# Output-gate projections of a gated recurrence as seven-product blocks of head pairs

## The chip, the cores and the metric

One of a Trainium2 chip's cores runs the kernel. TensorE (PE) multiplies, VectorE (DVE), ScalarE (ACT) and GpSimd (POOL) work on elements, SyncE (SP) and others issue the DMA transfers; each engine runs its own queue in order, and the engines wait for each other by semaphores. The metric is the device time of one execution in microseconds (us).

## The reference, cut to what matters

A residual block for 1024 tokens and 1024 channels: attention over 8 heads of 64 and a gated recurrence over 4 heads of 128 run side by side on the same normalised input, are merged by sigmoid gates, and an MLP follows.

```python
xn = rmsnorm(x, norm1_g)
q_sb, k_sb, v_sb, f_raw, i_hg, q_hg, g_hg, gate_sb, gate_hg = split(xn @ w_in)
o_sb = stick_breaking_attention(q_sb, k_sb, v_sb)
f = lb + (1 - lb) * sigmoid(f_raw)
k_hg = (1 - lb) * sigmoid(-f_raw)
o_hg = hgrn2_chunkwise(silu(q_hg), k_hg, i_hg, log(f))     # 4 heads of 128
o_hg = rmsnorm(o_hg, hg_norm_g)                            # per head
o_hg = merge_heads(o_hg) * silu(g_hg)                      # the output gate
g_a = sigmoid(gate_sb + b_a); g_b = sigmoid(gate_hg + b_b)
merged = g_a * (o_sb @ w_o_sb) + g_b * (o_hg @ w_o_hg)
h = x + merged @ w_out
h = h + square(relu(rmsnorm(h) @ w_ff1)) @ w_ff2
out = rmsnorm(h, final_g)
```

The change concerns `g_hg`, the last 512 of the recurrence's columns of `w_in`, and where its product with the head outputs is made.

## The kernel before, in words

**Numbers.** Every float32 operand of a product is split in two, a high part (a rounding copy on ScalarE, L148) and the rest (a subtraction on VectorE, L153). A product is three matmuls: high by high, high by low, low by high (`three`, L121). A matmul here has 128 rows of weights, 128 columns and 512 tokens. In names an `h` at the end is the high, an `l` the low part, `r` the raw weights as loaded. L161 is a multiplication on VectorE (`mul`), L1087 an addition, L1090 a subtraction, L124 a transpose on PE.

**Stages.** Normalisation and first projections (to about 60 us), attention (to 318), the recurrence (to 592), the rest of `o_sb @ w_o_sb` (to 615), the gates stage with `o_hg @ w_o_hg` (to 745), `w_out`, then the MLP.

**Two lanes on PE.** What depends on other engines (attention's scores and values, the recurrence's levels) is written by hand in order and goes to the lane "main". Projections that only need the normalised input are jobs of a stream `st` and go to the lane "fill": `st.advance(n, upto)` emits n steps of six matmuls each between pieces of the main lane, up to job number `upto`. Within a lane the order is that of the code, and a fill step is held behind the main block of `AHEAD = 2` blocks before, so that it runs where the main lane would leave PE idle. When a job starts, `prefetch` splits the next job's weights and loads those of the job after it.

**The recurrence.** Head h has eight levels (`hg_levels(h)`): `sd`, the diagonal, then levels 0 to 6 with doubling blocks, scores `sl` on PE and scalings of `k`, `q` and the decay `pp` on VectorE. Its tail (`hg_tail(h)`) has six parts: transposes `pk`, chunk states `pkv`, two halves of the output `pho` with their norm (`hon`, through GpSimd's `hn_y`), and two transposes back, `pot`. Levels of head h and the tail of head h-1 take turns. After every one of these parts fill steps are emitted, `FILL = (3.75, 3.3, 2.8, 2.6, 3)` of them by head. The gate `g` of a head is a projection of its own in the fill (`pjg`, weights `wg0` to `wg3`): per half of 512 tokens 8 blocks of 128 channels, 24 matmuls, then a sigmoid (ACT) and a product (DVE). The tail's last step multiplies the transposed output by the norm's weight and by `g`.

**Seven products for a block.** The columns of `gate_sb` and `gate_hg` were already made in pairs as two by two blocks: columns (two groups of 128) by channels (two halves of 512) by tokens (two halves of 512). Instead of eight block products there are seven. Three use the normalised input itself (`raw_job(cb)`, in the fill: banks `pga` and `pgq`, weights `wga`; the results go to DRAM in `pd` and `gd`). Four use sums of the input's blocks and of the weights' blocks and come in the gates stage, where `GatePair` loads the raw columns (`wg0r` and so on), subtracts and splits them (`whig`, `wlog`, `tgh`, `tgl`), loads the stored products (`pr`, `yr`) and does x6, y5, x7 and y3 (banks `gX`, `gY`, twelve matmuls each) and two products with `w_o_hg` (`late_half`, `early_half`: bank `pyh`, on the split head outputs `ahgh`, `ahgl`): 72 matmuls for one of the eight pairs. The input's sums (`gs`, `gsh`, `gsl`, by `sum_forms`) are made while `o_sb @ w_o_sb` runs (`sb_job`: bank `pys`, weights `wo00` to `wo03`, and `asbh`, `asbl` the split attention outputs). Head outputs are split whole, 1024 tokens at a time, by `a_hg.put`.

**Order.** The queues' order on ACT and DVE is set by a scheduler, except where `turns` is on or `after` adds an edge: there it is the code's. Loads go to SP's queue in the code's order. Raw weights have two buffers (tag `raw`), as have the high and the low parts (`whi`, `wlo`): a load waits until an older one has been read.

Of the kernel before, what the change touches and what calls it, by code (L numbers as in the profile page):

```python
# [19 lines left out]
P = 128  # L20
# [19 lines left out]
def kernel(  # L40
# [119 lines left out]
    def mul(out, a, b):  # L160
        return nc.vector.tensor_tensor(out=out, in0=a, in1=b, op=ALU.mult)  # L161
# [288 lines left out]
    class Stream:  # L450
        def __init__(self, eager=False):
            self.eager = eager
            self.jobs = []
            self.pos = 0
            self.gen = None
# [5 lines left out]
        def _start(self):  # L461
            units, body = self.jobs[self.pos]
            for u in units:
                u.split()
            if (self.pos > 0 or self.eager) and not units[-1].late:
                self.prefetch()
            self.gen = body()

# [50 lines left out]
    def proj_jobs(group, acts):  # L519


        def body():
            for half in range(2):
                for name, unit, ep in group:
# [249 lines left out]
    hg_sum, hg_level = [None], [None]  # L774
# [46 lines left out]
    def hg_jobs(h):  # L821
        for key, c0, ep in (
            ("f", C_F, f_epilogue(h)),
            ("q", C_QH, silu_epilogue(h, "q")),
            ("g", C_GH, silu_epilogue(h, "g")),
        ):
            if key == "g" and h % 2 == 0:
                i_job(h)
            u = cols_unit(f"w{key}{h}", [(W_IN, c0 + h * P, P)])
            j_hg[h] = proj_jobs([(f"pj{key}{h}", u, ep)], xn)  # L830

# [40 lines left out]

    def hg_levels(h):
# [17 lines left out]
        def pairs_of(name, n, *products):  # L891
# [4 lines left out]
            hi_lo(h_, l_, t)  # L896
# [28 lines left out]
        yield  # L925
        for l in range(7):
# [54 lines left out]
            yield  # L981

    def hg_tail(h):
        dec, k, q, g, v, sc = (hg.pop((h, n)) for n in ("pp", "k", "q", "g", "v", "sc"))
# [11 lines left out]
        yield  # L996
# [22 lines left out]
        yield  # L1019
        ons = []  # L1020
        for half in range(2):
# [14 lines left out]
            mul(chunks(on), chunks(po), rstd.unsqueeze(2).to_broadcast([P, 4, P]))  # L1036
            ons.append(on)
            yield
        for half, cs in halves():
            open_block("main")  # L1040
            pot = bank(f"pot{h}_{half}")
            for j in range(4):
                js = slice(j * P, (j + 1) * P)
                transpose(pot[:, js], ons[half][:, js])
            nc.vector.scalar_tensor_tensor(
                out=g[:, cs],
                in0=pot,
                scalar=prm[:, HGN + h : HGN + h + 1],
                in1=g[:, cs],
                op0=ALU.mult,  # L1050
                op1=ALU.mult,
            )
            yield
        ohg[h] = g


    class Split:
# [28 lines left out]
    def add(out, a, b):  # L1086
        return nc.vector.tensor_tensor(out=out, in0=a, in1=b, op=ALU.add)  # L1087

    def sub(out, a, b):
        return nc.vector.tensor_tensor(out=out, in0=a, in1=b, op=ALU.subtract)  # L1090
# [6 lines left out]
    yd = [dram(f"yd{cb}", [P, 2, 512]) for cb in range(KT)]  # L1097

# [26 lines left out]
    class RawUnit(Unit):  # L1125
# [4 lines left out]
        def __init__(self, cb):  # L1130
            dmas = [
                [(0, P, W_IN[:, gate_cols(w, cb)].rearrange("(k p) c -> p k c", p=P))]
                for w in range(2)
            ]
            super().__init__(f"wga{cb}", dmas)
# [20 lines left out]
    raw_units = [RawUnit(cb) for cb in range(KT)]  # L1156

    def raw_job(cb):
        u = raw_units[cb]
# [12 lines left out]
        def body():  # L1172
            p1, p14, g1 = (half(f"{n}_{cb}") for n in ("p1", "p14", "g1"))
            ps, p4 = bank(f"pga{cb}"), bank(f"pgq{cb}")
            if cb >= 6:
                load_g1(cb - 6)
            yield from steps_of(ps, 0, 0, 0, 0, True)
            nc.scalar.copy(p1, ps)
            nc.scalar.dma_start(pd[cb][:, 0, :], p1)
            if cb == 0:  # L1180
                u.split_t()
            st.prefetch()
            yield from steps_of(p4, 1, 0, 1, 4, True)
            add(p14, p1, p4)
            if cb == 3 or cb == KT - 1:
                whole_input(1, int(cb == KT - 1))
            nc.gpsimd.dma_start(pd[cb][:, 1, :], p14)
            yield from steps_of(ps, 0, 4, 0, 4, False)
# [5 lines left out]
        return st.add([u], body)  # L1194
# [8 lines left out]
    WAIT = 5  # L1203
# [7 lines left out]
    def sum_forms():  # L1211
# [30 lines left out]
        gp[0].load()  # L1242
        gp[0].load_sums()
# [6 lines left out]
        yield from range(4)  # L1250
        gp[0].split()
# [31 lines left out]
    j_raw = []  # L1283
# [9 lines left out]
    class GatePair:  # L1293
        def __init__(self, cb):
            self.cb = cb

        def load(self):
            cb = self.cb
            self.raw = [
                wpool.tile([P, 1024], F32, tag="raw", name=f"wg{cb}r{i}") for i in range(2)  # L1300
            ]
            for i, s_, which in ((0, 0, 0), (0, 1, 1), (1, 1, 1)):
                load(
                    self.raw[i][:, s_ * 512 : (s_ + 1) * 512].rearrange("p (k c) -> p k c", k=4),
                    W_IN[i * 512 : (i + 1) * 512, gate_cols(which, cb)].rearrange(
# [3 lines left out]
            self.wo = half(f"wor{cb}")  # L1309
# [11 lines left out]
        def split(self, behind=None):  # L1321
            cb = self.cb
# [4 lines left out]
            h, l = (  # L1327
                wpool.tile([P, 1024], F32R, tag=t, name=f"{t}g{cb}") for t in ("whi", "wlo")
            )
            after(hi_lo(h, l, r1), behind)  # L1330
            self.w = {6: (h[:, s0], l[:, s0]), 3: (h[:, s1], l[:, s1])}
            sub(r0[:, s1], r1[:, s1], r0[:, s1])
# [866 lines left out]
```

## Time and profile before

| | us |
|---|---|
| median of 3 runs | 1455.01 |
| lowest, highest | 1454.86, 1455.98 |
| profiled execution | 1454.49 |
| its span | 1452.7 |
| TensorE busy | 1436.7 |
| VectorE busy | 1096.7 |
| ScalarE busy | 675.6 |
| GpSimd busy | 125.2 |

The granted TensorE clock is 0.998 of full. A row of a timeline is start, duration, engine, line, operation, the tiles written and read, shapes, and in brackets the idle time before and what ended it. Durations of neighbours overlap, so that a price is read from one start to the next. A row of waits is engine, tile, line, what released it, us in total, how many times, the longest. A row of windows is a stretch, its length, then for PE, weight load, VectorE, ScalarE and GpSimd the busy time and the number of instructions, then the clock, the share of DMA and GB/s.

### The profile page before, as it was taken

How to read it: one execution, taken by the hardware profiler on the slowest of the kernel's cores; microseconds unless marked ns; L12 is line 12 of the kernel's file. 1: busy time of each engine (PE TensorE's matmuls, PEld its weight loads, DVE VectorE, ACT ScalarE, POOL GpSimd, SP SyncE). 2: the span in 40 equal slices, each digit the busy share in tenths (PEclk: the TensorE clock that was granted, in tenths of full speed). 3: DMA queues.
4: the chain of work that ended last, by engine and by line, in shares of the span. 5: the costliest groups of instructions: out<-in, count | busy, mean ns of one | idle time of the engine just before them, and what ended most of it. 6: DMA issues, size and time to landing. Idle time of an engine off the chain costs nothing. (4 is left out here: it accounts for less than half of the span.)

```text
span 1452.7 us, 19895 instructions
## 1 busy us (share of the span) xinstructions
PE 1436.7 (99%) x7442; PEld 1219.9 (84%) x7442; DVE 1096.7 (75%) x1557; ACT 675.6 (47%) x1166; POOL 125.2 (9%) x319
## 2 busy tenths in 40 slices
PE   8999999999999999999999999999999999999997
PEld 8889988988898888888888877888888888888886
DVE  6699898799658788877777797766666757768765
ACT  7566666552323334432344764444444533523343
POOL 3021111000000012100010200000000000000041
PEclk9999999999999999999999999999999999999999
DMA  6144255001213249655489403444445974776734
GB/s 207 34 120 92 57 112 109 16 29 45 81 44 102 66 141 245 221 192 186 162 275 290 174 30 132 158 159 154 151 160 191 349 263 181 253 275 246 276 104 178
DMA packets 157736, 227.30 MB, mean 156 GB/s; under 512 B 25308, under 2 KB 92936, under 8 KB 157640
## 3 DMA queue, kind: packets, MB, share of 16 engines
q1 hardware_dynamic: 142664, 184.07, 37.7%
q0 software_dynamic: 11376, 35.40, 9.4%
q10 hardware_dynamic: 3600, 6.56, 1.2%
q8 instruction: 59, 0.97, 0.3%
q14 instruction: 37, 0.30, 0.1%
HBM read 163.34 MB, written 62.65 MB: 156 GB/s over the span
## 5 line engine op out<-in xcount | busy, mean ns | idle before, releaser
L148 ACT CAST whid<-w 128x1024 fp32r<-128x1024 f32 x31 | 32.6, 1053 | 154.0 <-PE pm L121 89.8
L694 DVE TENSOR_TENSOR_SCAN rm<-rm,bits 128x511 f32<-128x511 f32 (+7 forms) x72 | 87.1, 1218 | 14.4 <-ACT rm L672 12.8
L121 PE MATMUL pm<-wlod,sh 128*128 128x512 f32 x248 | 96.7, 390 | 0.0
L121 PE MATMUL pm<-whid,sl 128*128 128x512 f32 x248 | 96.5, 389 | 0.0
L121 PE MATMUL pm<-whid,sh 128*128 128x512 f32 x248 | 96.5, 389 | 0.0
L153 DVE TENSOR_TENSOR wlod<-w,whid 128x1024 fp32r<-128x1024 f32 x31 | 37.8, 1221 | 56.4 <-ACT whid L148 56.4
L121 PE MATMUL pm<-th,sh 128*128 128x512 f32 x200 | 77.8, 389 | 0.0
L121 PE MATMUL pm<-tl,sh 128*128 128x512 f32 x200 | 77.8, 389 | 0.0
L121 PE MATMUL pm<-th,sl 128*128 128x512 f32 x200 | 77.8, 389 | 0.0
L153 DVE TENSOR_TENSOR sl<-sa,sh 128x1024 fp32r<-128x1024 f32 x56 | 68.2, 1217 | 1.9 <-ACT sh L148 1.9
L148 ACT CAST wTh<-pw 128x128 fp32r<-128x128 f32 (+3 forms) x96 | 44.3, 486 | 50.0 <-PE pw L124 45.2
L148 ACT CAST sh<-sa 128x1024 fp32r<-128x1024 f32 x56 | 57.3, 1047 | 12.3 <-DMA sa<-ad 12.3
L153 DVE TENSOR_TENSOR wTl<-pw,wTh 128x512 fp32r<-128x512 f32 (+3 forms) x96 | 50.7, 547 | 9.9 <-ACT wTh L148 5.4
L121 PEld LDWEIGHTS pm<-wlod,sh 128*128 128x128 f32 x248 | 46.6, 188 | 10.5 <-DVE wlod L153 0.8
L121 PEld LDWEIGHTS pm<-whid,sh 128*128 128x128 f32 x248 | 46.5, 187 | 9.7
L121 PEld LDWEIGHTS pm<-whid,sl 128*128 128x128 f32 x248 | 46.6, 188 | 9.5
L1841 POOL TENSOR_SCALAR fss<-fss 128x1 f32<-128x1 f32 x8 | 4.4, 551 | 567.1 <-ACT fsc L1836 566.5
L161 DVE TENSOR_TENSOR bt<-bt,rm 128x511 f32<-128x511 f32 (+7 forms) x72 | 48.9, 685 | 4.5 <-ACT bt L675 0.3
L121 PE MATMUL pX<-sqh,t1l 128*128 128x512 f32 x128 | 50.0, 391 | 1.2 <-DVE t1l L153 1.2
L121 PE MATMUL pX<-sqh,t1h 128*128 128x512 f32 x128 | 50.2, 392 | 1.0 <-DVE a L1087 0.9
L121 PE MATMUL pX<-sql,t1h 128*128 128x512 f32 x128 | 50.0, 390 | 0.0
L672 ACT ACTIVATE rm<-z 128x511 f32<-128x511 f32 (+6 forms) x96 | 47.5, 502 | 5.2 <-DVE bt L161 1.8
(921 smaller groups left out, 4566.0 us busy)
## 6 DMA issues: line engine op xcount, KB each, us to landing
w<-in_w_ff_dram SPq DMA_DIRECT2D x72, 512.0 KB, 5.4
sa<-ad SPq DMA_DIRECT2D x56, 512.0 KB, 6.3
ad<-a SPq DMA_DIRECT2D x32, 256.0 KB, 4.2
ad<-s SPq DMA_DIRECT2D x16, 512.0 KB, 3.3
tw<-in_w_out_dram POOLq DMA_DIRECT2D x6, 1024.0 KB, 7.7
x<-in_x_dram SPq DMA_DIRECT2D x8, 512.0 KB, 9.7
xnl<-xnh POOLq DMA_DIRECT2D x8, 512.0 KB, 9.6
pr<-pd SPq DMA_DIRECT2D x8, 512.0 KB, 6.5
```

The lines of the kernel that those rows point to most:

```text
L121: return pe(nc.tensor.matmul(*a, **k))
L148: return in_turn("act", nc.scalar.copy(dst, src))
L153: nc.vector.tensor_tensor(out=dst, in0=src, in1=hi.bitcast(F32), op=ALU.subtract),
L161: return nc.vector.tensor_tensor(out=out, in0=a, in1=b, op=ALU.mult)
L672: nc.scalar.activation(rm[:, s0 + c0 - 1 : s0 + m - 1], z[:, c0:m], AF.Sigmoid, scale=-0.125)
L694: sc = nc.vector.tensor_tensor_scan(out=rr, data0=rr, data1=bits[:, 1024 - nk + a : 1024 - nk + b][:, ::-1], initial=rm[:, b : b + 1] if i ...
L1841: nc.gpsimd.tensor_scalar(out=ssq, in0=ssq, scalar1=1.0 / D, scalar2=EPS, op0=ALU.mult, op1=ALU.add)
```

## The change

The gates `g` of heads 0 and 1, and of heads 2 and 3, become two by two blocks like the others. Three of a pair's products are a raw job in the fill (`g_job(j)`: banks `pgawgg`, `pgqwgg`, weights `wgg`), four are x6, y5, x7 and y3 of an `HgPair` at the start of the gates stage (banks `gXh`, `gYh`, weights `wgh0r` and `wgh1r`). The sigmoid, the product with the projection and the product with the head's output `o` follow there, quarter by quarter, and then the split (`put`, by halves of 512 tokens). `hg_tail` ends on ScalarE with the norm's weight alone. `gates()` writes the order of the two head pairs and the first two gate pairs out by hand, with `turns` on. The fill is dealt out by `LEVEL_SHARE` and `TAIL_SHARE`, and `STEPS` steps for each head. The jobs' order is: g_job(0) behind head 1's f and q, two gate jobs behind head 2's, g_job(1) and the others behind head 3's; `sb_job` may begin in head 3's levels (`upto` is `j_sb[2]` there).

```diff
@@ hg_jobs
         for key, c0, ep in (
             ("f", C_F, f_epilogue(h)),
             ("q", C_QH, silu_epilogue(h, "q")),
-            ("g", C_GH, silu_epilogue(h, "g")),
         ):
-            if key == "g" and h % 2 == 0:
-                i_job(h)
...
+    LEVEL_SHARE = (4, 4.5, 4.5, 3.2, 3.2, 3.2, 2.6, 2.6)
+    TAIL_SHARE = (1.5, 2.5, 2, 2, 1.5, 1.5)
...
@@ hg_tail
-            nc.vector.scalar_tensor_tensor(
-                out=g[:, cs],
-                in0=pot,
-                scalar=prm[:, HGN + h : HGN + h + 1],
-                in1=g[:, cs],
-                op0=ALU.mult,
-                op1=ALU.mult,
+            nc.scalar.activation(
+                o[:, cs], pot, AF.Identity, scale=prm[:, HGN + h : HGN + h + 1]
             )
-            yield
-        ohg[h] = g
+            yield TAIL_SHARE[4 + half]
...
@@ class Split
-        def put(self, i, src, behind=None):
-            h, l = slot(f"{self.name}h{i}", F32R), slot(f"{self.name}l{i}", F32R)
-            after(hi_lo(h, l, src), behind)
-            self.t[i] = (h, l)
+        def put(self, i, src, half_=None):
+            if i not in self.t:
+                self.t[i] = tuple(slot(f"{self.name}{n}{i}", F32R) for n in "hl")
+            cs = slice(0, 1024) if half_ is None else slice(half_ * 512, (half_ + 1) * 512)
+            h, l = self.t[i]
+            hi_lo(h[:, cs], l[:, cs], src[:, cs])
...
-    def raw_job(cb):
-        u = raw_units[cb]
+    def raw_job(name, cols, pd, c11, begin=None, middle=None):
+        u = RawUnit(name, cols)
...
+    def g_job(j):
+        def c11(ps):
+            t = half(f"sg{j}")
+            nc.scalar.activation(t, ps, AF.Sigmoid)
+            mul(t, ps, t)
+            nc.scalar.dma_start(hgd[j], t)
+        return raw_job(f"wgg{j}", [g_cols(2 * j), g_cols(2 * j + 1)], hpd[j], c11)
...
     hg_jobs(1)
-    j_raw.append(raw_job(0))
+    j_fill = j_hg[1]
+    j_g.append(g_job(0))
     hg_jobs(2)
-    j_raw.append(raw_job(1))
-    j_raw.append(raw_job(2))
+    j_raw += [gate_job(0), gate_job(1)]
     hg_jobs(3)
-    j_raw += [raw_job(cb) for cb in range(len(j_raw), KT)]
+    j_g.append(g_job(1))
+    j_raw += [gate_job(cb) for cb in range(len(j_raw), KT)]
...
+    class HgPair(SumPair):
+        def __init__(self, j):
+            self.j = j
+            super().__init__(f"h{j}", [g_cols(2 * j + i) for i in range(2)])
+        def load_sums(self):
+            self.p, self.g11 = slot(f"prh{self.j}"), half(f"g11r{self.j}")
+            load(self.p.rearrange("p (k t) -> p k t", k=2), hpd[self.j])
+            load(self.g11, hgd[self.j])
+        def times(self, i, cs, t):
+            o = ohg[2 * self.j + i][:, cs]
+            mul(o, o, t)
+        def sigmoid(self, t):
+            g = half(f"gs{self.cb}")
+            act(nc.scalar.activation(g, t, AF.Sigmoid))
+            return g
+        def first_quarter(self):
+            self.times(0, slice(0, 512), self.g11)
+        def late_sigmoids(self):
+            self.s = [self.sigmoid(self.p[:, c : c + 512]) for c in (0, 512)]
+        def late_times(self):
+            for i, g in zip((1, 0), self.s):
+                t = self.p[:, (1 - i) * 512 : (2 - i) * 512]
+                mul(t, t, g)
+                self.times(i, slice(512, 1024), t)
+        def early_times(self):
+            g = self.sigmoid(self.u2)
+            mul(self.u2, self.u2, g)
+            self.times(1, slice(0, 512), self.u2)
+        def put(self, i, half_):
+            a_hg.put(2 * self.j + i, ohg[2 * self.j + i], half_)
...
     def gates():
+        h0, h1, v0, v1 = summed[:4]
+        turns.update(on=True, act=None, dve=None)
+        h1.load_sums()
+        h1.roomy, v0.roomy = ("whi", "wlo"), ("raw",)
+        h1.sums()
+        h0.first_quarter()
+        h1.casts()
+        v0.load()
+        v1.load()
+        v0.load_sums()
+        h1.first_quarter()
+        v0.sums()
+        h0.x6()
+        h0.put(0, 0)
+        h1.put(0, 0)
+        v0.casts()
+        h0.y5()
+        h0.y5_sum()
+        v1.sums()
+        h0.x7()
+        h0.x7_sums()
+        h0.late_sigmoids()
+        h1.x6()
+        h0.late_times()
+        h0.y3()
+        h0.y3_sum()
+        h0.put(1, 1)
+        h0.put(0, 1)
+        h1.y5()
+        h1.y5_sum()
+        h0.early_times()
+        h1.x7()
+        h1.x7_sums()
+        h1.late_sigmoids()
+        h0.put(1, 0)
+        v0.x6()
+        h1.late_times()
+        v1.load_sums()
+        v1.casts()
+        h1.y3()
+        h1.y3_sum()
+        v0.y5()
+        v0.y5_sum()
+        h1.put(1, 1)
+        h1.early_times()
+        v0.x7()
+        v0.x7_sums()
+        v0.x7_gates()
+        h1.put(0, 1)
+        h1.put(1, 0)
+        v0.y3()
+        turns["on"] = False
+        summed[4].load()
+        v1.x6()
+        v0.y3_sum()
+        v0.y3_gate()
+        v0.late_half()
+        v0.early_half()
...
-    FILL = (3.75, 3.3, 2.8, 2.6, 3)
+    STEPS = (28, 42, 40, 38, 19)
...
-        upto = (j_hg[2], j_hg[3], j_raw[5], j_sb[1], j_sb[3])[h]
+        upto = (j_hg[2], j_hg[3], j_raw[5], j_sb[2], j_sb[3])[h]
+        rate = STEPS[h] / (sum(LEVEL_SHARE) * (h < NHG) + sum(TAIL_SHARE) * (h > 0))
...
-        if h > 1:
-            a_hg.put(h - 2, ohg[h - 2], hg_level[0])
-    a_hg.put(NHG - 1, ohg[NHG - 1])
     st.finish(j_sb[3])
-    gates_in[1].load()
+    summed[1].load()
     gates()
```

The instructions move most on VectorE; three places of its order follow. In the changed file an addition is L1090, a subtraction L1093.

First, the end of attention. `wTl` are the split weights that attention's last values wait for, `rm` and `bt` are its scan, `sd` is head 0's first level. Before:

```order
L161 TENSOR_TENSOR sd_x<-k_2851,q_3070 128x1024
L694 SCALAR_TENSOR_TENSOR rm_3_3809<-rm_3_3809,bits 128x511
L161 TENSOR_TENSOR q_3070<-q_3070,pp_2850 128x512
L161 TENSOR_TENSOR bt_3_3808<-bt_3_3808,rm_3_3809 128x511
L153 TENSOR_TENSOR wTl_1_0_3829<-pw_2_0_3832,wTh_1_0_3828 128x3x128
L153 TENSOR_TENSOR sd_l<-sd_x,sd_h 128x1024
L153 TENSOR_TENSOR wq1l_3862<-wq1r_3680,wq1h_3861 128x1024
L161 TENSOR_TENSOR g_3772<-pjg_1_3775,g_3772 128x512
L153 TENSOR_TENSOR wTl_2_0_3783<-pw_4_0_3850,wTh_2_0_3782 128x4x128
L153 TENSOR_TENSOR wTl_2_4_3785<-pw_4_1_3857,wTh_2_4_3784 128x128
```

Now:

```order
L161 TENSOR_TENSOR sd_x<-k_2855,q_3074 128x1024
L698 SCALAR_TENSOR_TENSOR rm_3_3818<-rm_3_3818,bits 128x511
L161 TENSOR_TENSOR q_3074<-q_3074,pp_2854 128x512
L161 TENSOR_TENSOR bt_3_3817<-bt_3_3817,rm_3_3818 128x511
L153 TENSOR_TENSOR wTl_1_0_3838<-pw_2_0_3841,wTh_1_0_3837 128x3x128
L153 TENSOR_TENSOR sd_l<-sd_x,sd_h 128x1024
L790 TENSOR_SCALAR k_3779<-k_3779,oml 128x512
L793 TENSOR_SCALAR pp_3778<-pp_3778,oml,lb 128x512
L153 TENSOR_TENSOR wTl_2_0_3792<-pw_4_0_3861,wTh_2_0_3791 128x4x128
L153 TENSOR_TENSOR wTl_2_4_3794<-pw_4_1_3868,wTh_2_4_3793 128x128
```

The split of `wq1` and the product `g` have left this piece (`wq1l` stands 25 rows earlier, where `wf1l` stood), and head 1's `k` and `pp` are scaled here and once more ten rows earlier, since its f job comes one job sooner; two rows `wgg0r`, of 1024 and 512, stand there too.

Second, the end of head 3's levels (`sl_4`, then the scalings of level 5). Before:

```order
L974 COPY_PREDICATED sc_5506<-bits,sl_4_0_5910 128x512
L974 COPY_PREDICATED sc_5506<-bits,sl_4_1_5915 128x512
L1045 SCALAR_TENSOR_TENSOR g_4921<-pot_1_5940,prm,g_4921 128x512
L153 TENSOR_TENSOR asbl_6045<-osb_3310,asbh_6044 128x1024
L153 TENSOR_TENSOR wo00l_5968<-wo00r_5888,wo00h_5967 128x1024
L161 TENSOR_TENSOR k_5229<-k_5229,pp_5228 128x8x32
L161 TENSOR_TENSOR q_5339<-q_5339,pp_5228 128x8x32
L161 TENSOR_TENSOR pp_5228<-pp_5228 128x8
L161 TENSOR_TENSOR k_5229<-k_5229,pp_5228 128x8x32
L161 TENSOR_TENSOR q_5339<-q_5339,pp_5228 128x8x32
L161 TENSOR_TENSOR pp_5228<-pp_5228 128x8
L1087 TENSOR_TENSOR p_7_5947<-p_7_5946,pgq_5950 128x512
```

Now:

```order
L980 COPY_PREDICATED sc_5522<-bits,sl_4_0_5939 128x512
L980 COPY_PREDICATED sc_5522<-bits,sl_4_1_5944 128x512
L153 TENSOR_TENSOR gsl_5976<-gs_5930,gsh_5975 128x1024
L1090 TENSOR_TENSOR gs_5985<-xnl_537,xnl_569 128x1024
L161 TENSOR_TENSOR g1r_5899<-pys_0_5968,g1r_5899 128x512
L1093 TENSOR_TENSOR gs_5986<-gs_5985,xnl_217 128x1024
L161 TENSOR_TENSOR k_4935<-k_4935,pp_4934 128x8x32
L161 TENSOR_TENSOR q_5037<-q_5037,pp_4934 128x8x32
L161 TENSOR_TENSOR pp_4934<-pp_4934 128x8
L161 TENSOR_TENSOR k_4935<-k_4935,pp_4934 128x8x32
L161 TENSOR_TENSOR q_5037<-q_5037,pp_4934 128x8x32
L161 TENSOR_TENSOR pp_4934<-pp_4934 128x8
```

The splits of the attention output and of the first w_o_sb weights have moved to earlier rows, and the input's sums `gs` with their splits `gsl`, which came behind the levels, have moved in.

Third, the start of the gates stage; `o` are head outputs, `g11r` the stored quarter of the gate. Before:

```order
L1090 TENSOR_TENSOR wg0r_6339<-wg0r_6340,wg0r_6339 128x512
L153 TENSOR_TENSOR gsl_6386<-gs_6371,gsh_6385 128x1024
L153 TENSOR_TENSOR wol_6440<-wor_6344,woh_6439 128x512
L153 TENSOR_TENSOR tgl_6436<-wg0r_6339,tgh_6435 128x1024
L161 TENSOR_TENSOR g1r_6376<-pys_0_6415,g1r_6376 128x512
L1090 TENSOR_TENSOR wg4r_6492<-wg4r_6492 128x512
L161 TENSOR_TENSOR g1r_6413<-pys_0_6461,g1r_6413 128x512
L1090 TENSOR_TENSOR wg4r_6493<-wg4r_6493,wg4r_6492 128x512
L1090 TENSOR_TENSOR wg4r_6492<-wg4r_6493,wg4r_6492 128x512
L1087 TENSOR_TENSOR gu_6512<-pr_6346,gX_6499 128x512
L153 TENSOR_TENSOR wlog_6530<-wg4r_6493,whig_6529 128x1024
L153 TENSOR_TENSOR tgl_6535<-wg4r_6492,tgh_6534 128x1024
```

Now:

```order
L1093 TENSOR_TENSOR wgh1r_6356<-wgh1r_6356 128x512
L1093 TENSOR_TENSOR wgh1r_6357<-wgh1r_6357,wgh1r_6356 128x512
L1093 TENSOR_TENSOR wgh1r_6356<-wgh1r_6357,wgh1r_6356 128x512
L161 TENSOR_TENSOR o_4340<-o_4340,g11r_6175 128x512
L153 TENSOR_TENSOR wlogh_6370<-wgh1r_6357,whigh_6369 128x1024
L161 TENSOR_TENSOR g1r_6250<-pys_0_6319,g1r_6250 128x512
L153 TENSOR_TENSOR tglh_6374<-wgh1r_6356,tghh_6373 128x1024
L161 TENSOR_TENSOR o_5564<-o_5564,g11r_6362 128x512
L1093 TENSOR_TENSOR wg0r_6377<-wg0r_6377 128x512
L1093 TENSOR_TENSOR wg0r_6378<-wg0r_6378,wg0r_6377 128x512
L1093 TENSOR_TENSOR wg0r_6377<-wg0r_6378,wg0r_6377 128x512
L1090 TENSOR_TENSOR guh_6412<-prh_6174,gXh_6399 128x512
```

The first pair's rows were followed by the second pair's `wg4r`; now head pair 1's raw columns are subtracted and split, the first quarters of `o` multiplied and the first gate pair's `wg0r` subtracted before PE's first product `gXh` of the stage is used.

More of the change, by code (lines that the diff above doesn't have):

```diff
@@ L1241, in sum_forms @@
             yield
-        gp[0].load()
-        gp[0].load_sums()
+        summed[0].load()
+        summed[0].load_sums()
         for kp in range(2):
@@ L1249, in sum_forms @@
             yield
-        yield from range(4)
-        gp[0].split()
+        yield from range(3)
+        summed[0].split()
     def sb_job(cp):
@@ new lines, in split, with product, x6 @@
+        def split(self, behind=None):
+            self.sums()
+            self.casts(behind)
+        def product(self, i, ps, start):
+            open_block("fill")
+            wh, wl = self.w[i]
+            for k in range(4):
+                c = k % 2 * 512
+                xh, xl = (t[:, c : c + 512] for t in forms[i, k // 2])
+                ws = slice(k * P, (k + 1) * P)
+                three(ps, wh[:, ws], wl[:, ws], xh, xl, start and k == 0, k == 3, True)
+        def x6(self):
+            self.X = bank(f"gX{self.cb}")
+            self.product(6, self.X, True)
+            self.u2 = half(f"gu{self.cb}")
+            self.u2_sum = add(self.u2, self.p[:, 0:512], self.X)
@@ L1309, in load, with __init__ @@
+    class GatePair(SumPair):
+        def __init__(self, cb):
+            super().__init__(cb, [gate_cols(w, cb) for w in range(2)])
+        def load(self):
+            cb = self.cb
+            super().load()
             self.wo = half(f"wor{cb}")
```

230 lines of the change are left out of this document (127 added, 103 removed).

## The prediction

> **What bounds the kernel now.** I read the page's head first (span, busy shares, the 40 slices, the chain), then TensorE's waits, then windows by stage, and last the timelines of the three places that the change rewrites.
>
> ```profile
> span 1452.7 us, 19895 instructions
> PE 1436.7 (99%) x7442; PEld 1219.9 (84%) x7442; DVE 1096.7 (75%) x1557; ACT 675.6 (47%) x1166; POOL 125.2 (9%) x319
> PE   8999999999999999999999999999999999999997
> PE 39%; DVE 3%; ACT 1%; issue 0%; POOL 0%; POOLq 0%; ACTq 0%
> ...
> PE po L121 <- DVE wTl L153: 1.2, 3, 0.6
> ...
> 318.00:592.00 274.00, 274.00 (x1663) 236.38 (x1661) 208.55 (x405) 89.63 (x194) 24.74 (x35) 1.00 0.36 105
> ...
> 318.00:380.00 62.00, 62.00 (x348) 52.12 (x347) 49.17 (x111) 18.33 (x29) 0.60 (x1) 1.00 0.20 60
> 380.00:440.00 60.00, 60.00 (x440) 54.96 (x439) 38.96 (x76) 15.18 (x46) 2.45 (x4) 1.00 0.15 45
> 440.00:504.00 64.00, 64.00 (x373) 54.30 (x372) 46.51 (x94) 19.83 (x43) 4.57 (x7) 1.00 0.27 83
> 504.00:566.00 62.00, 62.00 (x364) 52.67 (x363) 54.59 (x101) 26.54 (x50) 11.54 (x16) 1.00 0.61 171
> 566.00:592.00 26.00, 26.00 (x146) 22.34 (x144) 19.32 (x26) 9.76 (x26) 5.59 (x8) 1.00 0.87 250
> ...
> 592.00:615.00 23.00, 23.00 (x104) 19.04 (x103) 21.23 (x24) 11.61 (x14) 2.50 (x5) 1.00 0.64 211
> ...
> 615.00:745.00 130.00, 130.00 (x575) 107.67 (x574) 100.43 (x143) 42.79 (x56) 10.66 (x21) 1.00 0.58 192
> ```
>
> TensorE (PE) is busy in 99% of the span, no slice between the first and the last is below 9, and it holds most of the chain. In the windows (length, then busy time of PE, weight load, VectorE, ScalarE, GpSimd, then clock) it is busy without a gap through the recurrence (318 to 592) and the gates (615 to 745), at the full clock. So time is PE work, and a matmul removed is time removed unless PE then has to wait. The wait to watch is VectorE's (DVE): 76% busy over the recurrence (208.55 of 274), but 88% in the last head's levels (54.59 of 62) and 92% just ahead of the gates (21.23 of 23).
>
> **The saving.** A matmul costs its distance to the next one, not its shown duration:
>
> ```profile
> 615.18 0.39 PE L121 MATMUL gX<-gsh,whig 128*128 128x512 f32 x1
> 617.90 0.39 PE L121 MATMUL gY<-gsh,tgh 128*128 128x512 f32 x1
> 620.62 0.39 PE L121 MATMUL gX<-gsh,tgh 128*128 128x512 f32 x1
> L121 PE MATMUL pjg<-xnh,wg0h x16: 387/389/477, 294.7 to 311.5; 128*128 128x512 f32 x16
> ```
>
> The first rows of three products of twelve matmuls lie 2.72 us apart: 0.2267 us each, 2.72 for a product, 1.36 for a fill step of six. The four projections `pjg` leave, 4 heads x 2 halves x 24 = 192 matmuls; 2 pairs x 7 products x 12 = 168 come. 24 x 0.2267 = **5.44 us** saved. The program's order has just this difference, so that the change does not do what it says can be set aside.
>
> **What the change adds on other engines.** DVE goes from 1557 to 1587 instructions. Prices of a 512-wide and a 1024-wide operation, and of one that needs the result of the operation just ahead of it:
>
> ```profile
> 626.33 0.69 DVE L161 TENSOR_TENSOR pr<-pr,pyh 128x512 f32<-128x512 f32 x1
> 626.94 0.68 DVE L1090 TENSOR_TENSOR wg1r<-wg1r 128x512 f32<-128x512 f32 x1
> 635.08 1.22 DVE L153 TENSOR_TENSOR wlog<-wg1r,whig 128x1024 fp32r<-128x1024 f32 x1
> 636.22 1.22 DVE L153 TENSOR_TENSOR tgl<-wg1r,tgh 128x1024 fp32r<-128x1024 f32 x1
> 648.09 0.69 DVE L161 TENSOR_TENSOR gu<-gu,pyh 128x512 f32<-128x512 f32 x1
> 648.81 0.69 DVE L1087 TENSOR_TENSOR yr<-yr,gu 128x512 f32<-128x512 f32 x1
> ```
>
> Start to start that is 0.60, 1.14 and 0.72. Three places decide whether it reaches PE.
>
> *End of attention.* DVE has hardly a gap there, and PE already waits for `wTl`:
>
> ```profile
> 304.61 1.49 DVE L694 TENSOR_TENSOR_SCAN rm<-rm,bits 128x639 f32<-128x639 f32 x1 [0.25 <-ACT rm L672]
> 314.34 1.22 DVE L153 TENSOR_TENSOR wq1l<-wq1r,wq1h 128x1024 fp32r<-128x1024 f32 x1
> 315.47 0.68 DVE L161 TENSOR_TENSOR g<-pjg,g 128x512 f32<-128x512 f32 x1
> 316.07 0.88 DVE L153 TENSOR_TENSOR wTl<-pw,wTh 128x512 fp32r<-128x512 f32 x2
> 316.81 0.39 PE L121 MATMUL po<-wTl,V 128*128 128x256 f32 x1 [0.63 <-DVE wTl L153]
> 482.88 0.47 DVE L786 TENSOR_SCALAR k<-k,oml 128x512 f32<-128x512 f32 x1
> 483.27 0.53 DVE L789 TENSOR_SCALAR pp<-pp,oml,lb 128x512 f32<-128x512 f32 x1
> 483.73 0.74 DVE L1045 SCALAR_TENSOR_TENSOR g<-pot,prm,g 128x512 f32<-128x512 f32 x1
> ```
>
> Ahead of that `wTl` two subtractions for the first raw job come in (1.14 + 0.60) and twice the two scalings of head 1's gate (0.39 + 0.46 = 0.85 a time); two multiplications `g` leave (1.20), and the split `wq1l` leaves too (1.14), for an earlier place whose split `wf1l` has moved ahead in turn. 1.74 + 1.70 - 1.20 - 1.14 = +1.1 us, against a gap of 0.25 in the queue that can swallow some. PE's own rows ahead of it are the same in number, so the stall grows by 0.8 to 1.1, or by nothing if the subtractions slip into waits. I take **+0.8**.
>
> *Head 3's levels.* The w_o_sb job now begins in these levels and the summed inputs of the gates stage are formed there. From `sd` to the transposes `pk`, DVE gains five operations of 1024 (5.7) and four of 256 (0.34 each, rows below: 1.35) and loses four of 512 (1.20 + 2 x 0.66): +4.5 us; PE gains two steps of fill, 2.7. DVE comes 1.8 us later against PE than now.
>
> ```profile
> 563.68 1.15 PE L121 MATMUL sl<-q,k 128*64 128x64 f32 x16
> 564.40 0.42 DVE L161 TENSOR_TENSOR k<-k,pp 128x256 f32<-128x256 f32 x1 [1.03 <-PE sl L121]
> 564.74 0.42 DVE L161 TENSOR_TENSOR q<-q,pp 128x256 f32<-128x256 f32 x1
> ...
> 566.25 0.93 PE L124 MATMUL pk<-ident,k 128*128 128x128 f32 x7
> ```
>
> The first half of `k` is ready at 564.82, `pk` starts at 566.25: 1.43 us of slack, and DVE has a gap of 1.03 ahead. Both together hide it; slack alone leaves 0.4. Bounds 0 to 1.8, taken **+0.4**.
>
> *Start of the gates stage.* The first seven-product blocks must be summed, gated and split before w_o_hg's first product `pyh` can use them. Now DVE waits there for loads:
>
> ```profile
> 613.09 0.69 DVE L1090 TENSOR_TENSOR wg4r<-wg4r 128x512 f32<-128x512 f32 x1 [0.63 <-DMA wg4r<-in_w_in_dram]
> 615.85 1.29 DVE L1090 TENSOR_TENSOR wg4r<-wg4r,wg4r 128x512 f32<-128x512 f32 x2 [1.47 <-DMA wg4r<-in_w_in_dram]
> ...
> wg4r<-in_w_in_dram SPq DMA_DIRECT2D x3, 256.0 KB, 3.7
> ```
>
> From the first row of `wgh1r` to the split `ahgl` that `pyh` needs last, the new order has 51 operations of 512 and 6 of 1024: 51 x 0.60 + 6 x 1.14 = 37.4, and about ten of them follow their own producer, +1.2: 38.6. PE has 13 products ahead of `pyh`, and the third head's rows of `pyh` come half a product later: 35.4 + 1.4 = 36.8. DVE's queue begins 2.1 us before PE's first product, if the loads allow what they allow now (613.09 against 615.18). 38.6 - 2.1 = 36.5 against 36.8: covered by a hair. What waits behind a late load there is everything: `wgh1r` is the head of DVE's queue, and its raw buffers come free only when head pair 0's splits have read them; on SP the later loads (the stored partial products, the gates' columns) stand behind it. Lower bound 0, upper 3.4 (next part); near the lower end, since the rows at 0.60 are the rule: **+0.4**.
>
> The rest costs nothing on the path. The last scaling of each head's output goes from DVE to ScalarE, 89.63 of 274 busy there. The 16 added DMA issues lie in queues for which PE never waits; without that cover one load is 3.7 us, the time for which `wg4r` is under way. Heads 0, 1 and 2 give up 3, 4 and 1 steps of fill; DVE is busy 79%, 65% and 73% in their windows (49.17 of 62, 38.96 of 60, 46.51 of 64), so that its gaps cover these 1.4 to 5.4 us; without them PE would wait as long.
>
> Sum: -5.44 + 0.8 + 0.4 + 0.4 = **-3.8**. The profiled run took 1454.49 (span 1452.7 and 1.8 around it), which gives 1450.7; the median of the runs shown is 0.5 above the profiled one, so on it 1455.0 - 3.8 = **1451.2**. With each place at its lower end -5.4 + 0 gives 1449.6; at -5.4 + 1.1 + 1.8 + 1.0 it is 1453.5. That is the likeliest case's own range.
>
> **Rivals.**
>
> *DVE paces the gates' start* (no change). If its operations there come at full duration, 51 x 0.684 + 6 x 1.22 = 42.2, less 2.1 is 40.1 against 36.8: PE waits 3.4 us, and with 1.8 in head 3 and 1.1 in attention the sum is -5.4 + 6.3 = +0.9, or -0.3 if head 3 stays at 0.6: 1454.7 to 1455.9. For it: the pairs that follow their producer do come at 0.72. Against: independent neighbours stand 0.60 apart (626.33 to 626.94). [...] Chance 0.15.
>
> *The work ahead of the gates has nowhere to go* (slower). From head 3's levels to the first product of the gates (504 to 615) DVE is busy 54.59 + 19.32 + 21.23 = 95.1 of 111 us, with 15.9 of gaps. PE's fill after head 3's tail shrinks from 102 matmuls (the w_o_sb products at 592 to 615) to 6, and in head 3 it grows by 18: 78 x 0.2267 = 17.7 us, so 93.3 are left. By the order some 12.1 us of DVE's work leave that stretch (head outputs are split later, raw sums earlier), so 83.0 stay. If the gaps stay as well, because GpSimd, ScalarE and loads make them, 83.0 + 15.9 is 5.6 more than 93.3; the gates' queue starts so much later, and at full durations (+3.4) `pyh` waits 9.0:
>
> ```profile
> DVE hon L161 <- POOL hn_y L239: 3.0, 2, 1.8
> DVE p L1087 <- issue: 2.6, 1, 2.6
> ```
>
> With attention's 0.8 that is 1455.0 - 5.4 + 9.8 = 1459.4. It makes the kernel slower from a delay of 5.4, measurably from 8.3. For it: DVE's waits in head 3's window (504 to 566, in us, times, longest) are partly on GpSimd's `hn_y`, which the change leaves as it is. Against: the 2.6 before `p` and the 1.03 at 564.40 wait for an issue and for PE itself, and those a late DVE swallows first. Chance 0.18.
>
> *PE gains more.* If a removed matmul is worth its shown 0.389, 24 x 0.389 = 9.3, less 1.6: 1447.3. Against it stands the row spacing. Chance 0.10.
>
> **How the numbers follow.** The forecast has 0.57. A measurement of this kernel tells 0.2% (2.9 us) from no change: faster means below 1452.1, slower above 1457.9. Of the forecast 0.50 lies below 1452.1 and 0.07 above; with the third rival faster is 0.60; same is 0.07 + 0.15 = 0.22; slower 0.18. The range goes from 1448.0 (half of the third rival left out) to 1458.5 (most of the second left out).
>
> **What would show it.** The step of the saving is right if `pjg` is gone, 5128 matmuls of 512 stand at 0.227 apart and the stages after the gates are as long as now. The three stalls should stand in PE's waits: `po` on `wTl` at about 1.4 longest, `pk` on `k` below 1, `pyh` on `ahgl` below 1. `pyh` waiting 3 us or more means the first rival; `gXh` waiting 4 us or more for `wlogh0` or `tglh0` means the second. The forecast is wrong if PE's waits between 298 and 660 us grow by more than 3 us, or by nothing at all.

## The result, and the profile after

| | us |
|---|---|
| changed kernel, median of 20 runs | 1457.9 (1456.06 to 1459.73) |
| kernel before, median of 20 runs beside them | 1455.17 (1453.88 to 1456.9) |
| ratio | 1.0019, 95% interval 1.0012 to 1.0026 |
| span of the profiled execution, before and after | 1452.7, 1456.1 |

The change makes the kernel slower by 2.7 us, clear of no change, where 3.8 us less were forecast. The time lies inside the range, on the wrong side of no change.

The head of the page after, in the order of the lines shown of before, and PE's waits from 298 to 660 us (engine, tile, line, releaser; us in total, how often, the longest):

```profile
span 1456.1 us, 19929 instructions
PE 1433.2 (98%) x7418; PEld 1215.7 (83%) x7418; DVE 1114.2 (77%) x1587; ACT 685.4 (47%) x1184; POOL 127.7 (9%) x321
PE   8999999999999899999999999999999999999997
PE 36%; DVE 4%; ACT 1%; issue 1%; DMA 1%; POOL 0%; POOLq 0%; SPq 0%; DVEq 0%; ACTq 0%
...
PE pgawga L121 <- ACT p_wga L1178: 4.8, 2, 4.3
PE po L121 <- DVE wTl L153: 1.6, 2, 1.3
PE gY L121 <- DVE pr L1090: 0.5, 1, 0.5
PE gXh L121 <- DVE guh L1090: 0.3, 1, 0.3
```

PE runs 24 matmuls fewer (7418 for 7442), is busy 3.5 us less, and the span is 3.4 us longer: the matmuls were saved, and nearly 7 us of idle time came in. One slice of the 40 in PE's row fell to 8; it is the 14th, 473 to 510 us. The loss in it, from 493 to 501 us, falls in head 2's last levels: head 3's first operation, `sd_x`, starts at 501.93. The largest wait is one that the prediction does not name: not VectorE, but ScalarE's copy `p_wga` of a raw job's first partial sum.

A raw job adds into one bank, `pgawga`, twice: first third, then ScalarE copies the bank to `p_wga`, then the second product goes to another bank, then the last third is added on top. That last third must wait for the copy. PE's timeline there:

```profile
493.38 0.39 PE L121 MATMUL pgqwga<-xnh,wga4t 128*128 128x512 f32 x1
498.05 0.79 PE L121 MATMUL pgawga<-xnh,wga4whi 128*128 128x512 f32 x1 [4.29 <-ACT p_wga L1178]
498.64 0.63 PE L121 MATMUL pgawga<-xnl,wga4whi 128*128 128x512 f32 x1
499.07 0.63 PE L121 MATMUL pgawga<-xnh,wga4wlo 128*128 128x512 f32 x1
...
501.98 0.50 PE L121 MATMUL pgawga<-xnh,wga4whi 128*128 128x512 f32 x1
```

From 493.38 to 498.05 are 4.67 us where neighbours stand 0.23 apart: 4.4 us of loss. The starts of the six matmuls behind it are 0.42 to 0.59 from one to the next, 1.4 us more. ScalarE's timeline tells why the copy was late:

```profile
495.37 0.62 ACT L148 CAST wga5t<-wga5r 128x512 fp32r<-128x512 f32 x1 [8.16 <-DVE wga5r L1093]
495.90 0.68 ACT L1052 ACTIVATE o<-pot,prm 128x512 f32<-128x512 f32 x1
496.48 1.03 ACT L148 CAST asbh<-osb 128x1024 fp32r<-128x1024 f32 x1
497.41 0.59 ACT L1178 COPY p_wga<-pgawga 128x512 f32<-128x512 f32 x1
```

ScalarE stood still for 8.2 us. For more than the last five of them the copy, three places further back in its queue, could have run, since the last matmul that it needs starts at 489.29. At the queue's head was the cast `wga5t`, the split of the next job's third weights, which waits for VectorE's subtractions of `wga5r`, and those for the load:

```profile
486.47 1.00 SPq L129 DMA_DIRECT2D wga5r<-in_w_in_dram  x2
...
493.39 1.22 DVE L1093 TENSOR_TENSOR wga5r<-wga5r,wga5r 128x1024 f32<-128x1024 f32 x1 [2.95 <-DMA wga5r<-in_w_in_dram]
494.65 0.69 DVE L1093 TENSOR_TENSOR wga5r<-wga5r 128x512 f32<-128x512 f32 x1
```

The load was issued at 486.47, when wga4's splits had freed the two raw buffers, and 1 MB took until 493.39. The next job's third weights were not needed before 506.2; the copy behind their cast was needed at 493.6.

The cast stands ahead of this copy in the kernel before too, and there PE does not wait:

```profile
509.62 1.50 SPq L129 DMA_DIRECT2D wga5r<-in_w_in_dram  x2
...
516.74 0.39 PE L121 MATMUL pga<-xnh,wga4whi 128*128 128x512 f32 x1
...
520.52 0.62 ACT L148 CAST wga5t<-wga5r 128x512 fp32r<-128x512 f32 x1 [2.89 <-DVE wga5r L1090]
...
521.99 0.58 ACT L1178 COPY p<-pga 128x512 f32<-128x512 f32 x1
...
524.31 0.39 PE L121 MATMUL pga<-xnh,wga4whi 128*128 128x512 f32 x1
```

There the load was issued 7.1 us before job wga4's first matmul; in the changed kernel it was issued 0.15 us behind it (486.47 against 486.32). New is not the order of this pair but how late the load comes.

### The profile page after: what moved, and what is told of

The parts are those of the page before. It is cut to its first block, busy times and chain, and to the rows that moved or that the text cites. A ratio compares the mean times of both kernels' runs of the same rounds, so it can differ in the third digit from the quotient of the medians.

```text
span 1456.1 us, 19929 instructions
## 1 busy us (share of the span) xinstructions
PE 1433.2 (98%) x7418; PEld 1215.7 (83%) x7418; DVE 1114.2 (77%) x1587; ACT 685.4 (47%) x1184; POOL 127.7 (9%) x321
```

## The experiments

Each edit is against the changed kernel unless it says otherwise. Ratios are to the kernel before, from runs on the same chip.

**An order on ScalarE, for one job and for all.** `prefetch` holds the cast of the next weights behind PE's last matmul, but the raw units' second split (`split_t`) behind nothing. The edit gives both an edge to the copy:

```diff
-        def prefetch(self):
+        def prefetch(self, behind=None):
...
-                nxt[0].split(hi_behind=lanes["fill"].last)
-                nxt[0].split_t()
+                nxt[0].split(hi_behind=behind or lanes["fill"].last)
+                nxt[0].split_t(behind)
...
-                hi_lo(*self.hl[1], self.raw[1][:, 512:])
+                hi_lo(*self.hl[1], self.raw[1][:, 512:], behind)
...
-            nc.scalar.copy(p1, ps)
+            cp = nc.scalar.copy(p1, ps)
...
-            st.prefetch()
+            st.prefetch(cp)
```

In one_copy_first only job wga4 passes `cp` on.

> The changed kernel with one edge on ScalarE: the cast wga5t stands behind the copy p_wga of job wga4 (in the changed kernel it stands ahead of it, waits for the load of wga5r until 495.37 us, and PE waits 4.3 us for the copy and then runs six matmuls at half speed, 5.8 us in all). Theory A (the order on ScalarE is the cause): the wait of pgawga falls from 4.8 to about 0.5, the span from 1456.1 to about 1450.3, the ratio to the kernel before goes from 1.0019 to about 0.998. Theory B (the raw jobs ask for their weights faster than the loads bring them, so PE must wait there in any order): the wait moves to the next product of the job wga5, the span stays above 1454.5, the ratio near 1.001.

> As one_copy_first, with the same edge in every raw job. Theory A: the second, smaller wait (0.7 us at 470, for the copy of job wga2 behind the cast wga3whi) goes too, 0.5 to 0.7 us below one_copy_first, ratio about 0.9975. Theory B: no difference to one_copy_first.

one_copy_first: 1454.03 us, ratio 0.9995 (0.9986 to 1.0003), span 1452.2. all_copies_first: 1451.69 us, ratio 0.9977 (0.9968 to 0.9986), span 1449.4. Their waits of PE, 298 to 660 us for the first and 290 to 660 for the second:

```profile
PE po L121 <- DVE wTl L153: 1.6, 2, 1.3
PE sl L121 <- DVE q L161: 0.9, 1, 0.9
PE pgawga L121 <- ACT p_wga L1178: 0.7, 2, 0.5
...
```

```profile
PE po L121 <- DVE wTl L153: 1.6, 2, 1.3
PE gY L121 <- DVE pr L1090: 0.5, 1, 0.5
PE gXh L121 <- DVE guh L1090: 0.3, 1, 0.3
```

The wait did not move to the next product of wga5, so theory B falls: the load is early enough for its own use. For one job the gain is 3.9 us of span, not 5.8: another wait, `sl` on `q` (0.9), showed up, and the small wait for the copy of wga2 stayed. With all copies in front both are gone, and the whole change is worth 3.3 us, close to what was forecast for it. There the copy runs at 488.22 and the cast at 491.71: the load still ends behind the copy, and it costs nothing.

**The same wait cured by the load.** The order on ScalarE stays; the raw tiles of wga5 get buffers of their own, so that its load waits for none.

```diff
             super().__init__(name, dmas)
+            if name == "wga5":
+                self.roomy = (0, 1)
```

> The changed kernel, its order on ScalarE left as it is there, but with the two raw tiles of wga5 in buffers of their own, so that their load need not wait until wga4's splits have been read. Theory A: the cast wga5t is not late any more, so its place in the queue costs nothing: the wait of 4.3 us is gone, ratio about 0.998 as with one_copy_first. Theory B gives the same here; a third theory (the bank copy itself is late because ScalarE is overloaded in head 3's levels) leaves the wait at 3 us or more.

1454.16 us, ratio 0.9993 (0.9984 to 1.0002), span 1451.8; no wait on `p_wga` at all. The cast runs at 490.78 and the copy at 492.83 in place of 495.37 and 497.41, still in the old order. ScalarE was thus never overloaded. The ratio misses the 0.998 that was expected, and the time is 2.5 us above that of all_copies_first, although the wait is gone there too. The table of stages below shows where the 2.5 us lie: outside the recurrence.

**The wait made in the kernel before.** One job of the kernel before gets the reverse order:

```diff
+            if cb == 5:
+                st.prefetch()
-            nc.scalar.copy(p1, ps)
+            cp = nc.scalar.copy(p1, ps)
+            if cb == 5:
+                after(cp, raw_units[6].t_cast)
...
-            st.prefetch()
+            if cb != 5:
+                st.prefetch()
```

> The kernel before, with the reverse edge in one job: on ScalarE the copy p of job wga5 stands behind the cast wga6t (there it stood ahead: copy at 534.30, cast at 540.94 us). Theory A (a cast that waits for a load holds the copy that PE waits for): PE's second third of wga5, now at 538.5, waits for the copy until about 542: 3 to 4 us of wait on p, up to 1.5 more for slow matmuls after it, ratio 1.002 to 1.004. If something else made the changed kernel's loss, nothing changes: ratio 0.999 to 1.001.

1458.53 us, ratio 1.0021 (1.0012 to 1.003). Its ScalarE and PE there:

```profile
542.08 0.62 ACT L148 CAST wga6t<-wga6r 128x512 fp32r<-128x512 f32 x1 [8.90 <-DVE wga6r L1090]
542.60 0.58 ACT L1181 COPY p<-pga 128x512 f32<-128x512 f32 x1
...
543.24 0.50 PE L121 MATMUL pga<-xnh,wga5whi 128*128 128x512 f32 x1 [2.19 <-ACT p L1181]
```

One cast in the wrong place, with nothing else of the change, makes the old kernel 3.5 us slower. The wait itself is shorter than expected (2.2 us); the slow matmuls behind it (clock at 0.50, last section) take their share.

**The saving alone.** The kernel before without the low part of the weights in head 3's and half of head 2's gate projection: 24 matmuls fewer.

```diff
-            three(ps, wh[:, c : c + P], wl[:, c : c + P], xh, xl, kt == 0, kt == nk - 1)
+            if lean:
+                matmul(ps, wh[:, c : c + P], xh, start=kt == 0, stop=False)
+                matmul(ps, wh[:, c : c + P], xl, start=False, stop=kt == nk - 1)
+            else:
+                three(ps, wh[:, c : c + P], wl[:, c : c + P], xh, xl, kt == 0, kt == nk - 1)
...
+                    lean = name == "pjg3" or name == "pjg2" and half == 0
```

> The kernel before, leaving out the low part of the weights in head 3's gate projection and in half of head 2's: 24 matmuls of 512 fewer, and no other part of the change. The price of the saving by itself: at the spacing of the rows 24 x 0.2267 = 5.4 us, ratio 0.9963; at the shown duration 9.3 us, ratio 0.9936; if the fill was cover that PE needs, less than 3 us, ratio above 0.998.

1449.34 us, ratio 0.9963 (0.9949 to 0.9976), 5.6 us. The spacing of the rows (5.4) is the price, not the shown duration (9.3), and the fill was no cover.

**The dealing of the fill.** First the new shares alone in the kernel before, each head's total kept; then, in the changed kernel, shares half way to the old even dealing.

```diff
+    STEPS = (30, 46.2, 39.2, 36.4, 18)
...
+        rate = STEPS[h] / (27.8 * (h < NHG) + 11 * (h > 0))
+        shares = {lev: iter(LEVEL_SHARE), tail: iter(TAIL_SHARE)}
...
-                    owed += FILL[h]
+                    owed += next(shares[g]) * rate
```

```diff
-    LEVEL_SHARE = (4, 4.5, 4.5, 3.2, 3.2, 3.2, 2.6, 2.6)
-    TAIL_SHARE = (1.5, 2.5, 2, 2, 1.5, 1.5)
+    LEVEL_SHARE = (3.75, 4, 4, 3.35, 3.35, 3.35, 3, 3)
+    TAIL_SHARE = (2.2, 2.7, 2.5, 2.5, 2.2, 2.2)
```

> The kernel before with the fill dealt by the new shares, the totals of each head as before (30, 46.2, 39.2, 36.4, 18 steps); nothing else of the change. The scheduler then puts the cast wga7t ahead of the copy p of job wga6. Theory A: a wait of PE on that copy if the load of wga7r is late, 0 to 4 us, and none elsewhere: ratio 1.000 to 1.003. The rival that the new shares starve the late levels: several waits of PE on sl or pk in the levels 5 and 6, 3 us or more in sum. The rival that the shares are a gain by themselves: ratio below 0.998.

> The changed kernel, without the edge on ScalarE, with shares half way between the old even dealing and the new one (levels 3.75, 4, 4, 3.35, 3.35, 3.35, 3, 3; tail 2.2, 2.7, 2.5, 2.5, 2.2, 2.2; the steps of each head unchanged). The cast wga5t still stands ahead of the copy of job wga4, and wga4t ahead of that of wga3. If the place in the queue alone decides, PE waits at both, 4 us and more each: ratio above 1.002. If place and pace decide together (the copy is late only where the raw jobs follow each other faster than one load of 1 MB, some 7 us, and the splits after it allow), the slower pace shortens the wait on wga4 to less than 3 us: ratio 0.998 to 1.001.

Alone: 1454.97 us, ratio 0.9997 (0.9989 to 1.0006), and no new wait on PE. The shares are neither gain nor loss by themselves; a cast ahead of a copy stands there too (`wga7t` ahead of wga6's, 544.82 and 546.30), but in time. Half way: 1451.84 us, ratio 0.9976 (0.9967 to 0.9985), with the cast still ahead of the copy of wga4:

```profile
481.02 1.85 SPq L129 DMA_DIRECT2D wga5r<-in_w_in_dram  x2
...
490.52 0.62 ACT L148 CAST wga5t<-wga5r 128x512 fp32r<-128x512 f32 x1 [2.83 <-DVE wga5r L1093]
491.05 1.05 ACT L148 CAST asbh<-osb 128x1024 fp32r<-128x1024 f32 x1
492.00 0.57 ACT L1178 COPY p_wga<-pgawga 128x512 f32<-128x512 f32 x1
```

The order is that of the changed kernel, but the load is issued 5.4 us earlier (481.02 for 486.47; job wga4 starts at 486.58), the copy is done in time, and PE waits for it nowhere. Place and pace decide together: a cast in front with an early load (here, in own_buffers and in the kernel before) costs nothing, nor does a load that ends behind the copy when the cast stands behind it too (all_copies_first). Both cures at once:

> half_shares and the edges of all_copies_first together. Both remove the same wait, by the load's time and by the order. If that wait was the whole of the loss, together they give no more than each alone: ratio 0.9970 to 0.9985. If each cures a loss of its own, the gains add: ratio below 0.9960.

1450.79 us, ratio 0.9974 (0.9964 to 0.9985). The gains do not add, so it was one loss; this version, all_copies_first and half_shares beat both kernels and cannot be told apart.

**Stage by stage.** PE's rows cut each profiled execution into stages: from attention's first `z` to its last `po` on `wTl`, from there to the recurrence's last `pot`, and from there to the last `pyh`. The last column is everything before the first `z` and behind the last `pyh`. All in us:

| | attention | recurrence | gates | the rest |
|---|---|---|---|---|
| before | 268.0 | 272.9 | 153.6 | 758.3 |
| changed kernel | 268.7 | 274.4 | 155.0 | 758.0 |
| one_copy_first | 268.7 | 270.0 | 155.0 | 758.5 |
| all_copies_first | 268.7 | 267.4 | 155.0 | 758.4 |
| own_buffers | 268.7 | 267.5 | 155.2 | 760.4 |
| half_shares | 268.7 | 268.3 | 154.0 | 758.1 |
| half_shares_copies_first | 268.7 | 267.8 | 154.1 | 759.3 |
| before_less_24 | 268.0 | 267.4 | 153.6 | 758.6 |
| before_cast_first | 268.0 | 277.0 | 153.6 | 759.8 |

Own buffers take 6.9 us off the recurrence, all copies in front 7.0: both cure the whole loss. That own_buffers is slower all the same comes from the rest, where no edit changes PE's work and which differs by up to 2.4 us between these profiles; why it does is not shown. Against before, the recurrence of the cured kernel is 5.5 us shorter, as it is without any other part of the change in before_less_24.

**The smaller waits.** The other places where PE waits, starting from all_copies_first: the two subtractions `wgg0r` behind attention's last `wTl`; then also two exchanges in the order of `gates()`; then the first exchange alone.

```diff
-            sub(rb, ra, rb)
+            after(sub(rb, ra, rb), turn_lo[0] if self.name == "wgg0" else None)
...
-        v0.sums()
         h0.x6()
+        v0.sums()
...
         h1.y3()
-        h1.y3_sum()
         v0.y5()
         v0.y5_sum()
+        h1.y3_sum()
```

(The first also needs `prefetch` to be called later in the job ahead, so that the last `wTl` is already written.)

> all_copies_first with the two subtractions wgg0r of the first raw job behind attention's last wTl on VectorE. The prediction's term of 0.8 us for the end of attention: the wait of po for wTl goes from 1.3 back to about 0.6 (before: 0.6), 0.7 us less, ratio about 0.9972 against 0.9977. If that wait has another cause it stays at 1.3.

> attention_freed and, at the start of the gates stage, head pair 0's first sum ahead of the subtractions wg0r and the first gate pair's y5 sum ahead of head pair 1's y3 sum. The waits of gXh on guh (0.35) and of gY on pr (0.47) go: 0.8 us less than attention_freed, span about 1447.9, ratio about 0.9967. If VectorE is simply too full there, the waits only move to another bank or to pyh and the time stays that of attention_freed.

> all_copies_first with only the first of the two exchanges at the start of the gates stage (head pair 0's first sum ahead of the subtractions wg0r). The wait of gXh on guh (0.35) goes; if VectorE has room behind it, the time falls by 0.3, ratio 0.9970 to 0.9980; if it has none, pyh waits for ahgl or ahgh, and the time is that of all_copies_first or up to 1 us more.

attention_freed: 1452.65 us, ratio 0.9981 (0.9972 to 0.9989). all_places: 1453.97 us, ratio 0.9992 (0.9984 to 1.0001). first_sum_ahead: 1451.78 us, ratio 0.9978 (0.997 to 0.9987). None is faster than all_copies_first. PE's waits of all_places, 298 to 660 us:

```profile
PE sl L121 <- DVE q L161: 0.9, 2, 0.6
PE pyh L121 <- ACT ahgh L148: 0.9, 1, 0.9
PE pyh L121 <- DVE ahgl L153: 0.6, 1, 0.6
PE po L121 <- DVE wTl L153: 0.3, 1, 0.3
PE pgawgg L121 <- DVE wgg0wlo L153: 0.3, 1, 0.3
PE gY L121 <- DVE pr L1092: 0.2, 1, 0.2
```

`po` does fall from 1.3 to 0.3, as it should if the subtractions were its cause, but other rows shift with them and `sl` waits for `q` (0.9). At the gates' start the waits of `gXh` and `gY` shrink and `pyh` waits in their place: VectorE has little room there (busy 28.53 of the 30 us from 602 to 632 in the changed kernel), so that the two exchanges together mostly choose which bank is late. In first_sum_ahead `gXh` no longer waits and `gY` waits 0.8 in place of 0.5.

## Why the prediction was wrong

- **The saving** of 5.44 us held: 5.6 alone in before_less_24, whose recurrence is 5.4 shorter.
- **End of attention**, forecast +0.8. PE's first `wTl` matmul in the timelines after:

```profile
302.81 1.20 DVE L1093 TENSOR_TENSOR wgg0r<-wgg0r,wgg0r 128x1024 f32<-128x1024 f32 x1
304.73 0.68 DVE L1093 TENSOR_TENSOR wgg0r<-wgg0r 128x512 f32<-128x512 f32 x1
...
317.51 0.39 PE L121 MATMUL po<-wTl,V 128*128 128x256 f32 x1 [1.34 <-DVE wTl L153]
```

  1.34 against 0.63, +0.7: the count of operations in VectorE's queue was right, and with the two subtractions moved the wait falls to 0.3 (attention_freed).
- **Head 3's levels**, forecast +0.4 on `pk`: no wait there. VectorE's gap of 1.03 is gone and the slack ahead of `pk` fell from 1.43 to 0.53 us (`k` ready at 566.49, `pk` at 567.02): the two together hid it, as the prediction said they might.
- **Start of the gates**, forecast +0.4 on `pyh`. The place was right, the tile was not: `pyh` had its split in time, but two products had to wait until VectorE had read the bank that they add to:

```profile
600.86 0.39 PE L121 MATMUL gYh<-gsh,tglh 128*128 128x512 f32 x1
601.52 0.50 PE L121 MATMUL gXh<-gsh,tghh 128*128 128x512 f32 x1 [0.27 <-DVE guh L1090]
...
625.90 0.39 PE L121 MATMUL gX<-gsh,tgl 128*128 128x512 f32 x1
626.77 0.50 PE L121 MATMUL gY<-gsh,whig 128*128 128x512 f32 x1 [0.48 <-DVE pr L1090]
```

  Less the usual 0.23, the distances 0.66 and 0.87 are 0.4 and 0.6 us: 1.0 in place of 0.4 (the stage as a whole is 1.4 longer). That this and `pk` miss by about as much in opposite directions is luck.
- **"The rest costs nothing on the path"** is the step that failed. ScalarE was set down as cover because it was busy 89.63 of 274 us, and of the loads only the added ones were looked at, as lying in queues for which PE never waits. A share says how much an engine has to do, not what stands at the head of its queue. At the head of ScalarE's stood a cast that waited for a load, and PE waited for the copy behind it. The order alone would not have told, since the kernel before has the same pair in the same order; the load had to be followed to SP's queue and to the buffers that it waits for, as was done for `wgh1r` at the gates. It cost 4.4 us of wait, 1.4 of slow matmuls and 0.5 for the copy of wga2: some 6 us, which turn -3.8 into +2.7. By stages it is 7.0 us (recurrence of 274.4 against 267.4 with all copies in front).
- **The rivals.** Two were about VectorE at the gates, and neither came: `pyh` waits for nothing, `gXh` 0.3 us. The slower one had the right sign and the wrong mechanism, and since the range goes above the first rival's 1455.9 only for its sake, that it holds the result is luck. The third, a matmul worth its shown 0.389 us, falls with before_less_24 (5.6 us, not 9.3). The test written down for a wrong forecast, PE's waits between 298 and 660 us growing by more than 3, did catch it: they went from 0.9 (`po` alone) to 7.2.
- With the wait taken out, the terms of the sum give the time: all_copies_first is 3.3 us faster where 3.8 were forecast. By stages that is 0.7 more in attention, 5.5 less in the recurrence and 1.4 more at the gates.

## What to carry to other kernels

An engine that runs in order and is idle half the time (ScalarE here, busy 47% of the span) can still be the bound: look in its queue for an instruction that waits for a load, and for what stands behind it that the busy engine needs soon. An edge that keeps a prefetch's work behind the copy of the current job cost nothing here at either pace tried, and it decides between 0.2% slower and 0.2% faster. When jobs are moved or the fill is dealt out anew, follow each job's load too: buffers come free at another time relative to their use (7.1 us before the job's start in the kernel before, 0.15 us behind it now), although nothing in the load changed. And where two versions with the same cure differ in time, compare them stage by stage before blaming the cure.

## What the runs showed of the hardware

In two of the runs PE's granted clock stood at a half for about 3.4 us, at waits of 4.29 us (changed kernel) and 2.19 us (before_cast_first). Windows of the changed kernel (length, then busy PE, weight load, VectorE, ScalarE, GpSimd, then the clock, DMA, GB/s):

```profile
495.00:496.00 1.00, 0.00 (x0) 0.00 (x0) 0.34 (x1) 0.63 (x2) 0.00 (x0) 1.00 0.00 0
497.00:498.00 1.00, 0.00 (x0) 0.00 (x0) 0.46 (x1) 1.00 (x3) 0.00 (x0) 0.75 0.12 22
498.00:499.00 1.00, 0.95 (x2) 0.83 (x3) 1.00 (x2) 1.00 (x2) 0.00 (x0) 0.50 0.80 232
500.00:501.00 1.00, 1.00 (x4) 0.35 (x3) 1.00 (x3) 0.00 (x0) 0.00 (x0) 0.54 0.50 185
501.00:502.00 1.00, 1.00 (x17) 0.93 (x17) 1.00 (x3) 0.00 (x0) 0.00 (x0) 1.00 0.00 0
```

And of before_cast_first, whose wait ended at 543.24:

```profile
543.00:544.00 1.00, 0.77 (x3) 0.67 (x4) 1.00 (x3) 0.87 (x6) 0.00 (x0) 1.00 0.92 270
544.00:545.00 1.00, 1.00 (x4) 0.74 (x3) 1.00 (x5) 1.00 (x5) 0.61 (x2) 0.50 0.98 292
...
547.00:548.00 1.00, 1.00 (x6) 0.83 (x5) 1.00 (x2) 0.12 (x1) 0.00 (x0) 0.80 1.06 344
```

Read as split between full and half speed, the windows with 0.75, 0.54 and 0.80 give an estimate of the ends of the slow stretch: in the changed kernel the clock was at a half from about 497.5 to 500.9, 3.4 us, of which PE had work for 2.9. In before_cast_first the same came with a wait of 2.2 us, and because the slow stretch began 0.8 us after the wait had ended, all of it hit work: half speed from 544.0 to 547.4. The wait of 1.34 us in the changed kernel (`po` at 317.51) left the clock at 1.00 in each window from 316 to 319. That the wait of 2.2 us is the cause rests on this one place. From 15 us after the start to 10 us before the end, the kernel before has no wait of PE above 0.9 us and no window of 1 us with a clock below 0.99, and the changed kernel has no slow window but those from 497 to 501. What makes the clock fall, and what ends the slow stretch, is not shown. With the slow matmuls, the loss of 4.4 us in the changed kernel came to 5.8.
